# Moving the high part of stationary weights by 64 bytes in SBUF in a four-layer hybrid encoder

## The chip, the cores and the metric

The kernel runs on one core of one Trainium2 chip, in one launch that computes the whole encoder. The metric is the device time of a launch in microseconds (us), lower is better. The core has five engines that run side by side: PE (TensorE, the matrix array), DVE (VectorE), ACT (ScalarE), POOL (GpSimd) and SP (SyncE, which here only issues transfers). PE reads two things from SBUF, the on-chip memory: the stationary operand, which a weight load (PEld in the profile) puts into the array, and the moving operand, which a matmul streams past it. Results go to PSUM.

## What is computed

Four layers over a sequence of 256 rows of width 1024 in fp32. Each layer has a token mixer, a cross-attention over 256 memory rows and an MLP, and after each of the three a LayerNorm of `alpha*h + y`. The mixer is a gated linear recurrence (RG-LRU) in layers 0 and 3, an RWKV-7 delta rule in layer 1 and chunked attention in layer 2. The reference, cut to the trunk:

```python
for i in range(DEPTH):                       # DEPTH = 4
    kind, j = i % N_MIXERS, i // N_MIXERS
    y = (rglru_block, rwkv7_time_mix, chunk_relpos_attention)[kind](h, ...)
    h = _layer_norm(DEEPNORM_ALPHA * h + y, ln_g[i, 0], ln_b[i, 0])
    y = memory_cross_attention(h, mem, mx_w_q[i], mx_w_kv[i], mx_w_o[i])
    h = _layer_norm(DEEPNORM_ALPHA * h + y, ln_g[i, 1], ln_b[i, 1])
    y = squared_relu_mlp(h, mlp_w1[i], mlp_w2[i])      # square(relu(x @ w1)) @ w2
    h = _layer_norm(DEEPNORM_ALPHA * h + y, ln_g[i, 2], ln_b[i, 2])
```

## The kernel before

**Split products.** The large products keep nearly fp32 accuracy with the matrix array's fast fp32r type: every operand x is split into a high part (x rounded to fp32r) and a low part (the rest). A product of two split operands is three matmuls: high by high, low by high, high by low.

**The weight stream.** Weights come from HBM in chunks of 128 partitions by up to 1024 columns. `Stream._dma` (L97) issues the transfer of a chunk into a `wraw` tile on SP's queue, in the order of use. `Stream._split` (L114) makes two tiles of it: `whi`, by a cast on ACT (L471), and `wlo`, by a subtraction on DVE (L472). The pool `hl` holds seven `whi` and seven `wlo` tiles. The instruction order is written out by hand in Python; there is no scheduler.

**Two kinds of product.** Where activations are stationary (`mm_piece`, L289 to L291), the weights move: 512 columns of `whi` or `wlo` a matmul (504 or 336 in the RG-LRU), and every matmul loads 128 columns of activations. Where weights are stationary (`gemm_t` at L347, by `wt_piece`, L310 and L311), the activations move. The tile `ht` holds the transposed activations, first the high parts of both row halves, then the low parts. L310 loads 128 columns of `whi` and streams 512 columns: four runs of 128, high and low parts together. L311 loads 128 columns of `wlo` and streams 256: two runs of 128, the high parts. One after the other they are a **pair**; `gemm_t` makes four chunks into 32 pairs, in groups of 16 (8 and 4 where other work stands between). It serves seven of the eight blocks of the first MLP product in each layer, half of the query product of each cross-attention, and three sixths of the attention's projection: 35 calls, 1120 pairs. In an MLP block the 32 pairs are followed by 48 matmuls of the second MLP product with moving weights (L289 to L291). `wt_steps` (L330) also has stationary weights, for the keys of the memory: it takes 256 columns in every matmul.

**Homes.** By the home of a tile I mean its byte address in a partition. In the built program before, `whi`, `wlo`, `ht`, the activations of the MLP, the memory tiles and nearly all other operands of the fast matmuls have the home 224 modulo 256. Slices begin at multiples of 512 bytes, so that the operands that PE reads together begin at the same place modulo 256. Some small tiles (`mhalf`, `rc`) are wider than their use to keep it so. SBUF is nearly full at the widest stage.

Of the kernel before, what the change touches and what calls it, by code (L numbers as in the profile page):

```python
# [7 lines left out]
F32 = mybir.dt.float32  # L8
F32R = mybir.dt.float32r
# [7 lines left out]
T = 256  # L17
# [3 lines left out]
CT = 126  # L21
# [16 lines left out]
STP = 2  # L38
RW_B = 16
RC_P = 262  # L40
RC_S = 320 + RW_B
# [25 lines left out]
class Stream:  # L67
# [29 lines left out]
    def _dma(self):  # L97
        if self.nd >= len(self.plan):
            return
        k, (name, idx, p, f, _) = self.k, self.plan[self.nd]  # L100
        t = k.raw_p.tile([128, 1024], F32, name="wraw", tag="wraw")
        src = k.I[name]
        for i in idx:
            src = src[i]
        for c in self._cols(self.nd, f):
            k.nc.sync.dma_start(t[:p, c], src[:, c])
        self.raw[self.nd] = t
        self.nd += 1
# [5 lines left out]
    def _split(self):  # L114
# [3 lines left out]
        while self.nd <= i:  # L118
            self._dma()
        _, _, p, f, whole = self.plan[i]  # L120
        raw = self.raw.pop(i)
        if whole:
            self.hl[i] = raw
            self.ns += 1
            return
        hi = k.hl_p.tile([128, 1024], F32R, name="whi", tag="whi")
        lo = k.hl_p.tile([128, 1024], F32R, name="wlo", tag="wlo")
# [30 lines left out]

    def take(self, name, idx, p, f, whole=False):
        key = (name, tuple(idx), p, f, whole)  # L160
        if self.k.dry:
            self.plan.append(key)
            return 0
        i = self.pos
        assert self.plan[i] == key, (self.plan[i], key)
        self.pos += 1
        while self.ns <= i:
            self._split()
        return i
# [74 lines left out]
class Kern:  # L244
# [9 lines left out]

    def chunks(self, name, idx, n, p, f):
        if self.gb_due is not None:
            self.gb_due -= 1
            if self.gb_due == 0:
                if self.ln_i == 0:
                    for t in range(2):  # L260
                        self.nc.sync.dma_start(self.h[t], self.I["x"][t * 128:(t + 1) * 128, :])
                self.load_gb()
        return [self.st.take(name, (*idx, q), p, f) for q in range(n)]

# [82 lines left out]
    def gemm_t(self, name, idx, x, banks):  # L347

        ch = self.chunks(name, idx, 4, 128, 1024)
        for m in range(2):  # L350
# [37 lines left out]
    def resid(self, t, nh, acc):  # L388
# [5 lines left out]
        if nh == 0:  # L394
            self.bn[t] = self.sm.tile([128, 2, 6], F32, name="bnst", tag="bnst")
        self.nc.vector.bn_stats(out=self.bn[t][:, nh, :], in_=h[:, sl])
# [160 lines left out]
    def cross(self, l, left):  # L557

        nc, tc = self.nc, self.tc
        with tc.tile_pool(name="cr", bufs=1, reuse_waits="tile") as p:  # L560
# [4 lines left out]
            P, PT, o = {}, {}, {}  # L565
            sums = [self.sm.tile([128, 4], F32, name="ssum", tag="ssum") for _ in range(2)]

# [232 lines left out]
    def lru(self, l, j):  # L800
# [3 lines left out]
        with self.tc.tile_pool(name="lru", bufs=1, reuse_waits="tile") as p:  # L804
# [13 lines left out]
            def x_piece(i):  # L818
                for t, a in self.gemm(*half_in(1, i), 4, self.hT, 128, LW[i]):
                    if i == 0 and t == 0:  # L820
                        x0 = p.tile([128, 2, LW[0]], F32, name="xn", tag="C")
                    s = x0[:, t, :] if i == 0 else gn[t][:, 1008:] if i == 2 else p.tile([128, LW[1]], F32, name="xn", tag=f"B{t}")
                    nc.scalar.copy(s, a[:, :LW[i]])
# [72 lines left out]
            def decay(g):  # L896
                n = tiles[g]
                a, h = ri[g][:, 0], ri[g][:, 1]
                a2 = p.tile([CT, 4, T], F32, name="a2", tag="C")[:, :n, :]
                nc.scalar.activation(a, a, AF.Exp)  # L900
# [261 lines left out]
    def rwkv(self, l, j):  # L1162
# [6 lines left out]
        R2 = r2.enter_context(tc.tile_pool(name="rwb", bufs=1, reuse_waits="tile"))  # L1169
        rc = R2.tile([128, RC_P + 24], F32, name="rc")  # L1170
        nc.sync.dma_start(rc[:, :RC_P], self.I["rw_const"][:, :RC_P])
        cumM, cumX, w3 = rc[:, 0:128], rc[:, 128:256], rc[:, 256:262]
        two = lambda P, n: [P.tile([128, D], F32, name=f"{n}{t}", tag=f"{n}{t}") for t in range(2)]
        r, k, a, s = two(R1, "r"), two(R2, "k"), two(R2, "a"), two(R2, "s")
# [3 lines left out]
        rkrow = R2.tile([128, D], F32, name="rkrow", tag="rkrow")  # L1178
        Dc = R2.tile([128, 8, 8], F32, name="Dc")[:, :3]
        state = [R2.tile([128, 4, 64], F32, name=f"st{f}") for f in range(2)]  # L1180
        hv = lambda x: x.rearrange("p (a b) -> p a b", b=64)
# [458 lines left out]
        def gn(t, f):  # L1640

            cs = slice(f * 512, (f + 1) * 512)
            y = r[t][:, cs]
            mn = self.sm.tile([128, 8], F32, name="gmn", tag="gmn")
            vr = self.sm.tile([128, 8], F32, name="gvr", tag="gvr")
            sq = R2.tile([128, 512], F32, name="gsq", tag=("ptmp", "pi")[f])
# [51 lines left out]
        if not GNP:  # L1698

            S.activation(self.sm.tile([128, 1], F32, name="gone", tag="gone"), self.mhalf[:, 0:1], AF.Sqrt, scale=-1.0)  # L1700
        run(1, elim(0), gram(0, 0), gram(0, 1), pre(1))
        lnxg = self.gb_p.tile([128, D], F32, name="lnxg", tag="g")
        lnxb = self.gb_p.tile([128, D], F32, name="lnxb", tag="b")
# [67 lines left out]
    def run(self):  # L1771
# [14 lines left out]
        with ExitStack() as ctx:  # L1786
# [6 lines left out]
            self.ht_p = P("ht", 1)  # L1793
            self.sm = P("sm", 4)
            self.acc_p = P("acc", 4, space=PSUM)
            self.mm_p = P("mm", 2, space=PSUM)
# [3 lines left out]
            if not self.dry:  # L1800
                make_identity(nc, self.ident[:, :])
            self.mhalf = self.c_p.tile([128, 120], F32, name="mhalf")
            nc.vector.memset(self.mhalf, -0.5)
# [185 lines left out]
```

## Time and profile before

| | |
|---|---|
| median of 3 runs | 1785.25 us |
| lowest and highest | 1781.33 and 1785.4 us |
| the profiled execution | 1786.16 us |
| its span, first to last instruction | 1784.4 us |
| its mean granted TensorE clock | 0.987 |

The profile is of one execution. A row of its groups has source line, engine, operation, result and operands with their shapes, count, then the busy time in us and the mean time of one in ns, then the idle time of the engine just before. A matmul's duration there has its way through the array in it, so matmuls that follow each other overlap; how fast they follow is read from their starts in the timeline. The granted clock is a share of the full 2.4 GHz: 1.00 is that level and 0.50 is 1.2 GHz.

### The profile page before, as it was taken

Reading aid. Unit: us, or ns where it says so; the run is one execution under the profiler, and the core shown is the slowest. Engines: PE = TensorE matmul, PEld = TensorE weight load, DVE = VectorE, ACT = ScalarE, POOL = GpSimd, SP = SyncE. Lnnn points to the kernel's source line nnn. Section 1 sums busy time; section 2 is a strip of 40 time slices with the busy share of each in tenths; the row PEclk is TensorE's granted clock in tenths of the full one; section 3 lists DMA queues with packets and bytes.
Section 4 is the critical chain, followed back from the end, with each engine's and each line's share of the span. In section 5 each row is a group of like instructions: output and inputs, shape, how many; then the busy total and the mean of one; then the engine's idle time right before and its main releaser. Section 6 shows DMA issues by size and latency. Waiting matters only on the chain.

```text
span 1784.4 us, 25405 instructions
## 1 busy us (share of the span) xinstructions
PE 1723.6 (97%) x9944; PEld 1432.5 (80%) x9944; DVE 1248.9 (70%) x1795; ACT 852.4 (48%) x1268; POOL 55.5 (3%) x70
## 2 busy tenths in 40 slices
PE   8989999999999989999999999999999999999998
PEld 6788988888777656888887888888888787988886
DVE  6767676667578698786666666876667777676665
ACT  5754544444444133644443544645444674544442
POOL 3000000000000001000000000000000000000000
PEclk9899999999999999999999999999999999999999
DMA  7365555556342223455556634446554645536552
GB/s 265 102 213 173 189 189 189 189 189 204 95 146 72 96 84 129 143 187 200 188 190 202 238 107 141 148 150 224 188 190 158 225 138 181 201 130 225 190 189 94
DMA packets 92277, 301.11 MB, mean 169 GB/s; under 512 B 11770, under 2 KB 19962, under 8 KB 92028
## 3 DMA queue, kind: packets, MB, share of 16 engines
q1 hardware_dynamic: 92156, 299.48, 49.7%
q8 instruction: 78, 1.28, 0.3%
q14 instruction: 43, 0.35, 0.1%
HBM read 298.40 MB, written 1.05 MB: 168 GB/s over the span
## 4 chain that ended last, share of the span: by engine, by line
PE 80%; DVE 10%; ACT 4%; DMA 3%; issue 2%; POOL 0%; SPq 0%; DVEq 0%; ACTq 0%
PE acc L291 12%; PE acc L290 12%; PE acc L289 12%; PE tp L310 5%; PE mm L310 5%; PE acc L310 4%; PE acc L533 4%; PE acc L330 4%; PE tp L311 3%; PE mm L311 3%; PE acc L203 2%; PE tp L368 2%; DVE wlo L472 2%; PE acc L311 2%; PE mm L502 1%
## 5 line engine op out<-in xcount | busy, mean ns | idle before, releaser
L472 DVE TENSOR_TENSOR wlo<-wraw,whi 128x1024 fp32r<-128x1024 f32 (+4 forms) x505 | 591.8, 1203 | 145.8 <-ACT whi L471 134.0
L471 ACT CAST whi<-wraw 128x1024 fp32r<-128x1024 f32 (+4 forms) x505 | 507.3, 1035 | 220.4 <-PE acc L291 147.5
L289 PE MATMUL acc<-whi,ahi 128*128 128x512 f32 x512 | 200.3, 391 | 0.0
L291 PE MATMUL acc<-whi,alo 128*128 128x512 f32 x512 | 199.7, 390 | 0.0
L290 PE MATMUL acc<-wlo,ahi 128*128 128x512 f32 x512 | 199.3, 389 | 0.0
L289 PE MATMUL acc<-whi,ht 128*128 128x512 f32 (+2 forms) x368 | 143.3, 389 | 5.5 <-ACT whi L471 5.5
L290 PE MATMUL acc<-wlo,ht 128*128 128x512 f32 (+2 forms) x368 | 141.5, 384 | 3.9 <-DVE wlo L472 3.9
L291 PE MATMUL acc<-whi,ht 128*128 128x512 f32 (+2 forms) x368 | 141.5, 385 | 1.7 <-DVE ht L372 1.7
L310 PE MATMUL tp<-ht,whi 128*128 128x512 f32 x384 | 136.7, 398 | 0.0
L310 PE MATMUL mm<-ht,whi 128*128 128x512 f32 x384 | 136.5, 398 | 0.0
L310 PE MATMUL acc<-ht,whi 128*128 128x512 f32 x352 | 126.0, 400 | 2.2 <-DVE qkT L1011 2.2
L291 PEld LDWEIGHTS acc<-whi,alo 128*128 128x128 f32 x512 | 96.1, 188 | 20.9
L289 PEld LDWEIGHTS acc<-whi,ahi 128*128 128x128 f32 x512 | 96.1, 188 | 20.1
L290 PEld LDWEIGHTS acc<-wlo,ahi 128*128 128x128 f32 x512 | 96.2, 188 | 19.2
L311 PE MATMUL tp<-ht,wlo 128*128 128x256 f32 x384 | 107.9, 281 | 0.0
L311 PE MATMUL mm<-ht,wlo 128*128 128x256 f32 x384 | 107.8, 281 | 0.0
L311 PE MATMUL acc<-ht,wlo 128*128 128x256 f32 x352 | 98.6, 280 | 0.0
L759 DVE TENSOR_TENSOR rel<-mm,rel 128x256 f32<-128x256 f32 x48 | 18.6, 425 | 110.4 <-ACT rel L758 110.4
L763 ACT CAST ahi<-rel 128x512 fp32r<-128x512 f32 x56 | 34.8, 622 | 110.2 <-DVE rel L762 110.2
L289 PEld LDWEIGHTS acc<-whi,ht 128*128 128x128 f32 x368 | 70.6, 192 | 20.1 <-ACT whi L471 6.2
L310 PEld LDWEIGHTS tp<-ht,whi 128*128 128x128 f32 x384 | 72.2, 188 | 18.0
L310 PEld LDWEIGHTS mm<-ht,whi 128*128 128x128 f32 x384 | 72.2, 188 | 17.6
(395 smaller groups left out, 3318.3 us busy)
## 6 DMA issues: line engine op xcount, KB each, us to landing
wraw<-in_w SPq DMA_DIRECT2D x256, 512.0 KB, 4.7
wraw<-in_w_kv SPq DMA_DIRECT2D x64, 512.0 KB, 4.6
wraw<-in_w_q SPq DMA_DIRECT2D x32, 512.0 KB, 4.3
wraw<-in_w_co SPq DMA_DIRECT2D x32, 512.0 KB, 4.6
wraw<-in_lru_in SPq DMA_DIRECT2D x31, 504.0 KB, 4.8
wraw<-in_ca_qkv SPq DMA_DIRECT2D x24, 512.0 KB, 4.8
wraw<-in_lru_out SPq DMA_DIRECT2D x20, 512.0 KB, 6.0
ln_gt<-in_ln_g SPq DMA_DIRECT2D x12, 512.0 KB, 6.5
```

Source lines behind the costliest of these rows:

```text
L203: return f(*a, **k)
L289: nc.tensor.matmul(acc[:, :w], lhsT=a, rhs=wh[:p, ws], start=s, stop=False)
L290: nc.tensor.matmul(acc[:, :w], lhsT=a, rhs=wl[:p, ws], start=False, stop=False)
L291: nc.tensor.matmul(acc[:, :w], lhsT=b, rhs=wh[:p, ws], start=False, stop=e)
L310: self.nc.tensor.matmul(four, lhsT=wh[:, ws], rhs=xy, start=s, stop=False)
L311: self.nc.tensor.matmul(four[:, :2], lhsT=wl[:, ws], rhs=x, start=False, stop=e)
L330: self.nc.tensor.matmul(a, lhsT=w[:, ws], rhs=v, start=s and i == 0, stop=e and i == 2)
L368: self.nc.tensor.transpose(dst_ps[:n, j * p:(j + 1) * p], s, self.ident[:p, :p])
L471: self.nc.scalar.copy(hi, src)
L472: self.nc.vector.tensor_tensor(out=lo, in0=src, in1=hi.bitcast(F32), op=ALU.subtract)
L533: nc.tensor.matmul(a, lhsT=u, rhs=w[:, ws], start=s, stop=e)
L763: nc.scalar.copy(hi[:, sl, :], r)
```

## The change

`take`, `chunks` and the plan of the stream carry a new number, `shift`. `gemm_t` passes 16, all others 0. `_split` makes the `whi` tile 1088 columns wide in place of 1024 and takes the 1024 columns from `shift` on: with 16 fp32 columns that is 64 bytes further. `wlo` is left as it is. A `whi` tile is then 4352 bytes, 17 times 256, so the tiles' own homes stay at 224 modulo 256. In the built program `whi` stands at 32 modulo 256 for the 140 chunks of `gemm_t` and at 224 for the others; `wlo`, `ht` and the rest of the fast operands stay at 224.

The seven wider tiles take 1792 bytes more in each partition. To make room, small tiles share homes: in the RG-LRU the tile `xn` of the first piece takes the home of `B0`, the next ones move to `B1` and `B2`, and `a2` takes the home of the gate weights `gw0`; in the RWKV layer the constants `rc` and the state share the tag `st` and the state is made later; `mhalf`, `Dc` and the LayerNorm statistics get smaller or fewer tiles; `ssum`, `gmn` and `gvr` take the tags of other small tiles. `rc`, `Dc` and the state then stand at 96 modulo 256.

The diff:

```diff
--- before.py
+++ after.py
@@ -37,6 +37,7 @@
 ST0 = 3
 STP = 2
 RW_B = 16
+DCP = 32
 RC_P = 262
 RC_S = 320 + RW_B
 PE_SHARE = .4,.4,.4,.4
@@ -97,7 +98,7 @@
     def _dma(self):
         if self.nd >= len(self.plan):
             return
-        k, (name, idx, p, f, _) = self.k, self.plan[self.nd]
+        k, (name, idx, p, f, *_) = self.k, self.plan[self.nd]
         t = k.raw_p.tile([128, 1024], F32, name="wraw", tag="wraw")
         src = k.I[name]
         for i in idx:
@@ -117,13 +118,13 @@
         k, i = self.k, self.ns
         while self.nd <= i:
             self._dma()
-        _, _, p, f, whole = self.plan[i]
+        _, _, p, f, whole, shift = self.plan[i]
         raw = self.raw.pop(i)
         if whole:
             self.hl[i] = raw
             self.ns += 1
             return
-        hi = k.hl_p.tile([128, 1024], F32R, name="whi", tag="whi")
+        hi = k.hl_p.tile([128, 1088], F32R, name="whi", tag="whi")[:, shift:shift + 1024]
         lo = k.hl_p.tile([128, 1024], F32R, name="wlo", tag="wlo")
         w = f // 2
         if _pitch(w) == w or f <= 512:
@@ -156,8 +157,9 @@
         if not self.k.dry and self.ns == self.last + self.hl_bufs:
             self._split()
 
-    def take(self, name, idx, p, f, whole=False):
-        key = (name, tuple(idx), p, f, whole)
+    def take(self, name, idx, p, f, whole=False, shift=0):
+
+        key = (name, tuple(idx), p, f, whole, shift)
         if self.k.dry:
             self.plan.append(key)
             return 0
@@ -252,7 +254,7 @@
         self.st = Stream(self, [] if self.dry else plan, 4, 7)
 
 
-    def chunks(self, name, idx, n, p, f):
+    def chunks(self, name, idx, n, p, f, shift=0):
         if self.gb_due is not None:
             self.gb_due -= 1
             if self.gb_due == 0:
@@ -260,7 +262,7 @@
                     for t in range(2):
                         self.nc.sync.dma_start(self.h[t], self.I["x"][t * 128:(t + 1) * 128, :])
                 self.load_gb()
-        return [self.st.take(name, (*idx, q), p, f) for q in range(n)]
+        return [self.st.take(name, (*idx, q), p, f, shift=shift) for q in range(n)]
 
     def mm_piece(self, acc, chunks, lhs, p, w, kpc=2, kt0=0, start=True, stop=True, last=False, near=None, tail=None):
 
@@ -346,7 +348,7 @@
 
     def gemm_t(self, name, idx, x, banks):
 
-        ch = self.chunks(name, idx, 4, 128, 1024)
+        ch = self.chunks(name, idx, 4, 128, 1024, shift=16)
         for m in range(2):
             accs = [banks[m](), banks[m]()]
             self.wt_piece(accs, ch, x.both, m, last=m == 1)
@@ -392,7 +394,7 @@
             out=h[:, sl], in0=h[:, sl], scalar=ALPHA, in1=acc[:, :], op0=ALU.mult, op1=ALU.add
         )
         if nh == 0:
-            self.bn[t] = self.sm.tile([128, 2, 6], F32, name="bnst", tag="bnst")
+            self.bn[t] = self.bn_p.tile([128, 2, 6], F32, name="bnst", tag=f"bnst{t}")
         self.nc.vector.bn_stats(out=self.bn[t][:, nh, :], in_=h[:, sl])
 
     def ln(self, t, aside=None):
@@ -563,7 +565,7 @@
             q = [pair([128, 4, T], f"qh{g}", f"ql{g}") for g in range(2)]
             self.kv_hl = (k, v) = pair([128, 8, T], "kh", "kl"), pair([128, 2, D], "vh", "vl")
             P, PT, o = {}, {}, {}
-            sums = [self.sm.tile([128, 4], F32, name="ssum", tag="ssum") for _ in range(2)]
+            sums = [self.sm.tile([128, 4], F32, name="ssum", tag="ss") for _ in range(2)]
 
             def take_over(i):
 
@@ -818,8 +820,8 @@
             def x_piece(i):
                 for t, a in self.gemm(*half_in(1, i), 4, self.hT, 128, LW[i]):
                     if i == 0 and t == 0:
-                        x0 = p.tile([128, 2, LW[0]], F32, name="xn", tag="C")
-                    s = x0[:, t, :] if i == 0 else gn[t][:, 1008:] if i == 2 else p.tile([128, LW[1]], F32, name="xn", tag=f"B{t}")
+                        x0 = p.tile([128, 2, LW[0]], F32, name="xn", tag="B0")
+                    s = x0[:, t, :] if i == 0 else gn[t][:, 1008:] if i == 2 else p.tile([128, LW[1]], F32, name="xn", tag=f"B{t + 1}")
                     nc.scalar.copy(s, a[:, :LW[i]])
                     nat[i, t] = s
                     if i and t == 0:
@@ -896,7 +898,7 @@
             def decay(g):
                 n = tiles[g]
                 a, h = ri[g][:, 0], ri[g][:, 1]
-                a2 = p.tile([CT, 4, T], F32, name="a2", tag="C")[:, :n, :]
+                a2 = p.tile([CT, 4, T], F32, name="a2", tag="gw0")[:, :n, :]
                 nc.scalar.activation(a, a, AF.Exp)
                 nc.scalar.activation(a2, a, AF.Square)
                 nc.vector.scalar_tensor_tensor(out=h, in0=a2, scalar=1.0, in1=h, op0=ALU.add, op1=ALU.mult)
@@ -1167,17 +1169,17 @@
         r1, r2 = ExitStack(), ExitStack()
         R1 = r1.enter_context(tc.tile_pool(name="rwa", bufs=1, reuse_waits="tile"))
         R2 = r2.enter_context(tc.tile_pool(name="rwb", bufs=1, reuse_waits="tile"))
-        rc = R2.tile([128, RC_P + 24], F32, name="rc")
+        rc = R2.tile([128, RC_P], F32, name="rc", tag="st")
         nc.sync.dma_start(rc[:, :RC_P], self.I["rw_const"][:, :RC_P])
         cumM, cumX, w3 = rc[:, 0:128], rc[:, 128:256], rc[:, 256:262]
+        Dc = R2.tile([128, DCP], F32, name="Dc")[:, :24].rearrange("p (c q) -> p c q", c=3)
         two = lambda P, n: [P.tile([128, D], F32, name=f"{n}{t}", tag=f"{n}{t}") for t in range(2)]
         r, k, a, s = two(R1, "r"), two(R2, "k"), two(R2, "a"), two(R2, "s")
         g2 = R1.tile([128, D], F32, name="g2")
         tg = R1.tile([128, T], F32, name="tg")
         bs = [R1.tile([128, 16], F32, name=f"bs{t}") for t in range(2)]
         rkrow = R2.tile([128, D], F32, name="rkrow", tag="rkrow")
-        Dc = R2.tile([128, 8, 8], F32, name="Dc")[:, :3]
-        state = [R2.tile([128, 4, 64], F32, name=f"st{f}") for f in range(2)]
+        state = []
         hv = lambda x: x.rearrange("p (a b) -> p a b", b=64)
         bc = lambda x, p=128: x.unsqueeze(2).to_broadcast([p, 8, 64])
         half = lambda c: slice(64 * c, 64 * c + 64)
@@ -1641,8 +1643,8 @@
 
             cs = slice(f * 512, (f + 1) * 512)
             y = r[t][:, cs]
-            mn = self.sm.tile([128, 8], F32, name="gmn", tag="gmn")
-            vr = self.sm.tile([128, 8], F32, name="gvr", tag="gvr")
+            mn = self.sm.tile([128, 8], F32, name="gmn", tag="nm")
+            vr = self.sm.tile([128, 8], F32, name="gvr", tag="rs")
             sq = R2.tile([128, 512], F32, name="gsq", tag=("ptmp", "pi")[f])
             V.tensor_reduce(mn, hv(y), AX.X, ALU.add)
             V.tensor_scalar(mn, mn, -1.0 / 64, None, ALU.mult)
@@ -1699,6 +1701,8 @@
 
             S.activation(self.sm.tile([128, 1], F32, name="gone", tag="gone"), self.mhalf[:, 0:1], AF.Sqrt, scale=-1.0)
         run(1, elim(0), gram(0, 0), gram(0, 1), pre(1))
+        st2 = R2.tile([128, 2, 4, 64], F32, name="st", tag="st")
+        state += [st2[:, f] for f in range(2)]
         lnxg = self.gb_p.tile([128, D], F32, name="lnxg", tag="g")
         lnxb = self.gb_p.tile([128, D], F32, name="lnxb", tag="b")
         nc.sync.dma_start(lnxg, self.I["rw_lnx_g"][j].partition_broadcast(128))
@@ -1792,6 +1796,7 @@
             self.gb_p = P("gb", 1)
             self.ht_p = P("ht", 1)
             self.sm = P("sm", 4)
+            self.bn_p = P("bn", 1)
             self.acc_p = P("acc", 4, space=PSUM)
             self.mm_p = P("mm", 2, space=PSUM)
             self.tp_p = P("tp", 2, space=PSUM)
@@ -1799,7 +1804,7 @@
             self.ident = self.c_p.tile([128, 128], F32, name="ident")
             if not self.dry:
                 make_identity(nc, self.ident[:, :])
-            self.mhalf = self.c_p.tile([128, 120], F32, name="mhalf")
+            self.mhalf = self.c_p.tile([128, 56], F32, name="mhalf")
             nc.vector.memset(self.mhalf, -0.5)
             self.hT = _LazyT(self)
             self.h = [self.c_p.tile([128, D], F32, name=f"h{t}") for t in range(2)]
```

On every engine the instructions stand in the same order before and after, with the same shapes (the one other width is `mhalf`'s, a memset of 120 columns that becomes 56). What differs in the built program beside addresses is a few waits that come from the shared homes: four on ACT before exponentials of the cross-attention, three on POOL in the RWKV layer, and one on SP. The one on SP stands in the second RG-LRU layer (layer 3), where SP's queue carries the gate weights `gw`, the memory `kT`, a LayerNorm's rows and then the weight chunks `wraw`. Before:

```order
L106 DMA wraw<-in_lru_in 128x1008 [waits DMAHW2_49,DVE_49]
L865 DMA gw<-in_lru_gw 128x1512 [waits PE_49] x2
L865 DMA gw<-in_lru_gw 128x2x504
L459 DMA kT<-in_memT 128x8x128
L459 DMA kT<-in_memT 128x8x128 [waits DMAHW3_49]
```

The same place on SP after:

```order
L107 DMA wraw<-in_lru_in 128x1008 [waits DMAHW2_49,DVE_49]
L867 DMA gw<-in_lru_gw 128x1512 [waits PE_49] x2
L867 DMA gw<-in_lru_gw 128x2x504 [waits PE_49]
L461 DMA kT<-in_memT 128x8x128
L461 DMA kT<-in_memT 128x8x128 [waits DMAHW3_49]
```

Nothing has moved; the third transfer of gate weights now waits for a matmul as the first two do. In the built program that is the last matmul of L622 in the cross-attention of layer 2.

## Rows read from the trace of the kernel before

**Rows 1.** The page's busy shares of the engines over the span.

```profile
PE 1723.6 (97%) x9944; PEld 1432.5 (80%) x9944; DVE 1248.9 (70%) x1795; ACT 852.4 (48%) x1268; POOL 55.5 (3%) x70
```

**Rows 2.** The page's chain that ended last, by engine.

```profile
PE 80%; DVE 10%; ACT 4%; DMA 3%; issue 2%; POOL 0%; SPq 0%; DVEq 0%; ACTq 0%
```

**Rows 3.** One MLP block, 379.4 to 401.6 us: busy time of each engine.

```profile
core 0: us, PE busy (x) PEld busy (x) DVE busy (x) ACT busy (x) POOL busy (x), PEclk, DMA share, GB/s
379.40:401.60 22.20, 22.20 (x114) 18.77 (x113) 13.71 (x17) 10.38 (x15) 0.00 (x0) 1.00 0.56 190
```

**Rows 4.** The page's groups of the pairs (busy us, mean ns of one | idle).

```profile
L310 PE MATMUL tp<-ht,whi 128*128 128x512 f32 x384 | 136.7, 398 | 0.0
L310 PE MATMUL mm<-ht,whi 128*128 128x512 f32 x384 | 136.5, 398 | 0.0
L310 PE MATMUL acc<-ht,whi 128*128 128x512 f32 x352 | 126.0, 400 | 2.2 <-DVE qkT L1011 2.2
```

**Rows 5.** PE's timeline in one MLP block: start us, duration us, instruction.

```profile
366.87 0.39 PE L290 MATMUL acc<-wlo,ahi 128*128 128x512 f32 x1
...
368.00 0.39 PE L310 MATMUL mm<-ht,whi 128*128 128x512 f32 x1
368.23 0.28 PE L311 MATMUL mm<-ht,wlo 128*128 128x256 f32 x1
368.34 0.40 PE L310 MATMUL mm<-ht,whi 128*128 128x512 f32 x1
368.57 0.28 PE L311 MATMUL mm<-ht,wlo 128*128 128x256 f32 x1
368.69 0.40 PE L310 MATMUL mm<-ht,whi 128*128 128x512 f32 x1
368.93 0.28 PE L311 MATMUL mm<-ht,wlo 128*128 128x256 f32 x1
369.05 0.40 PE L310 MATMUL mm<-ht,whi 128*128 128x512 f32 x1
369.29 0.28 PE L311 MATMUL mm<-ht,wlo 128*128 128x256 f32 x1
369.40 0.40 PE L310 MATMUL mm<-ht,whi 128*128 128x512 f32 x1
...
379.29 0.40 PE L289 MATMUL acc<-whi,ahi 128*128 128x512 f32 x1
...
390.23 0.39 PE L310 MATMUL mm<-ht,whi 128*128 128x512 f32 x1
```

**Rows 6.** PE's timeline, matmuls of 256 columns alone; 50 starts lie between.

```profile
178.38 0.28 PE L330 MATMUL acc<-memlo,whi 128*128 128x256 f32 x1
...
184.38 0.28 PE L330 MATMUL acc<-memhi,whi 128*128 128x256 f32 x1
```

**Rows 7.** Granted clock and busy time of 746 to 751 us.

```profile
746.00:751.00 5.00, 5.00 (x24) 4.97 (x24) 5.00 (x5) 3.07 (x4) 0.00 (x0) 0.50 0.51 154
```

**Rows 8.** PE's timeline there; 21 starts lie between the last two rows.

```profile
745.53 0.55 PE L622 MATMUL mm<-qh,vh 128*128 128x256 f32 x1 [1.45 <-DVE ql L372]
...
746.41 0.41 PE L622 MATMUL mm<-qh,vl 128*128 128x256 f32 x1
...
750.89 0.41 PE L622 MATMUL mm<-qh,vl 128*128 128x256 f32 x1
```

**Rows 9.** PE's timeline: the gate matmuls, plain fp32, four passes of 256 columns each.

```profile
1405.19 1.03 PE L877 MATMUL mm<-xc,gw 127*126 127x256 f32 x4
...
1415.62 1.03 PE L877 MATMUL mm<-xc,gw 127*126 127x256 f32 x4
```

**Rows 10.** SP's timeline in layer 3, and PE's in the cross-attention before.

```profile
1168.64 0.28 PE L622 MATMUL mm<-qh,vl 128*128 128x256 f32 x1
...
1386.99 1.62 SPq L865 DMA_DIRECT2D gw<-in_lru_gw  x3
```

## The prediction, made before the changed kernel ran

> **What bounds the kernel now.** I read the page's busy shares first, then its chain, then one MLP block by stages, then PE's timeline. PE is busy for 97% of the span, DVE for 70%, ACT for 48% [rows 1], and the chain that ended last is PE for 80% [rows 2]. The shares are averages, so the stage that the change touches must be read by itself. In an MLP block PE is busy for all of 22.20 us, while DVE needs 13.71, ACT 10.38 and the transfers 0.56 of the DMA engines' time [rows 3]. No other engine is near its limit there, and the pairs wait for almost nothing: 2.2 us in all in front of the 1120 L310 (384 and 384 and 352) [rows 4]. So in these stages the end moves by what PE's pace gains or loses, in full: a pair that gets 1 ns shorter is worth 1.1 us.
>
> The pace is in the starts [rows 5]. Matmuls of 512 moving columns with activations as weights follow each other 226 ns apart: five between 366.87 and 368.00. Then 32 pairs run from 368.00 to 379.29, 352.8 ns each. Their steps are not even: the first pair takes 0.34 us, the next 0.35, 0.36, 0.35. The 48 matmuls that follow take 10.94 us, 227.9 ns each, 1.9 ns over 226: the unevenness is carried into them for a little. Matmuls of 256 columns alone follow at 120.0 ns: 50 starts in 6.00 us [rows 6]. A pair is one of 512 and one of 256, so by these paces it should take 346 ns. It takes 352.8. **6.8 ns of a pair are lost to something that neither kind suffers alone.**
>
> What is it? At a granted clock of 0.50, the 1.2 GHz level, matmuls of 256 columns follow at 213.3 ns, 4.48 us for 21, with their weights loaded beside them as always [rows 7, 8]; PE had waited 1.45 us for DVE ahead of that stretch [rows 8]. Twice as fast would be 106.7 ns; at 1.00 it is 120.0. So 13.3 ns come on top at the full clock, and a fixed number of array cycles is not the reason, since at the lower clock it would then cost more, and it costs nothing. Something that does not get faster with the array is met only when columns stream at the full clock. The weight load that runs beside each matmul and reads SBUF at the same time is the candidate. If two readers meet, then it can matter where each stands, and in every fast matmul both now stand at the same home modulo 256.
>
> **The change part by part.**
>
> *The shift.* It touches one load out of two in a pair: the load of `whi`, which runs beside L311. The load of `wlo` beside L310 keeps its relation to `ht`. No row of before has a fast matmul whose load stands 64 bytes off, so its price has to be bounded. From below: half of the overhead cannot be touched, because it belongs to the load of `wlo`. The fastest that L311 could stream is 106.7 ns [rows 7, 8], with L310 at 226 [rows 5]: 333 ns a pair, 20 less than now, times 1120 is -22 us. A nearer row is the first pair of a group, which starts from an undisturbed stream and takes 340 ns [rows 5]: -12.8 x 1120 = -14.3 us. Nearer still is the pace of both kinds alone, 346 ns: -6.8 x 1120 = -7.6 us. From above: the loss could happen twice, 6.8 ns more, +7.6 us. I take 346 ns. The even streams are the commonest state in this trace, they come from readers that keep one relation from matmul to matmul, and the pairs differ from them in that their unequal lengths let the relation wander; a fixed quarter turn between `whi` and `ht` would keep the two from starting on the same place. I do not take 340: it is seen only where nothing lay before.
>
> *The carry into the MLP's second product.* If the pairs run evenly, the 1.9 ns on each of 48 matmuls go as well, 0.09 us a block, 28 blocks: -2.6 us at most [rows 5]. Part of it may be waiting of another kind, so I count a quarter, -0.6 us.
>
> *Writing and reading the shifted tile.* ACT's cast and DVE's subtraction write and read it in the same shapes. If they changed pace, the block has 8.5 us of room on DVE and 11.8 on ACT [rows 3]: nothing.
>
> *The shared homes.* All engines keep their order. The new waits name instructions of an earlier stage. The one on a queue that matters is SP's: the third load of gate weights at about 1387 us now waits for a matmul that started at 1168.64 us [rows 10], 218 us before, so neither it nor the memory's rows and the weight chunks queued behind it on SP start later. The waits on ACT and POOL are of the same kind, on uses at least a sub-layer back: nothing. If one of them were late, it would show as an idle time of the engine, and it would have to exceed a microsecond to be measured.
>
> *Sum.* -7.6 - 0.6 = -8.2 us from the profiled execution's 1786.2 us gives 1778.0. The median of the runs is 0.9 us lower than that execution, so against the median it is 1777.1.
>
> **The Trainium skill against this.** The trace says 120.0 ns at the full clock where the lower one would make it 106.7 [rows 6 to 8]. "TensorE: Matmul & The Clock Gate", in "Step-by-step: what each phase is for", says that PE has two independent read ports, so that loading the next weights takes no read bandwidth from the running matmul, and "SBUF — State Buffer", in "Who interferes with whom", that PE never waits on anyone. By that rule a home could not matter, and the sum would be nought. The rows do not decide it: an overhead at the full clock is there, but no row ties it to an address.
>
> **The rivals.**
>
> *No change.* The overhead belongs to swapping weights at the full clock and not to where they stand. For it: plain fp32 matmuls load the gate weights from homes that lie between 224 and 56 modulo 256 in the built program, against a moving operand at 224, and four passes take 1.03 us with either end [rows 9]. There the home is of no account. Against it: those passes stream 256 columns in some 215 ns, half the pace, where the overhead is not met either; and a cost of swapping would not explain why a pair of unequal lengths loses 6.8 ns more. The time is then the median's, 1785.3 us. This is also what the skill's rule gives.
>
> *More than forecast.* The load of `whi` no longer meets the stream at all: 340 ns or less, -14.3 us to -22 us, 1771 to 1763 us. For it: the first pair of a group does it [rows 5]. Against it: a stream that passes 512 bytes of weights at twice their speed crosses their place somewhere in any case.
>
> *Slower.* The same home is the good relation: both readers start together, the stream is ahead at once and stays clear for the longest time. With `whi` 64 bytes ahead, the stream runs into the load just after the start of L311, in every pair. For it: 226 and 120 ns, the even paces, are all reached with equal homes [rows 5, 6]. Against it: the pairs have equal homes as well and are uneven. The price is one more loss a pair: it decides from the point where L311 takes over 120 ns as a mean, which no other work hides since PE is never idle there, and 6.8 ns x 1120 is +7.6 us: 1792.9 us.
>
> **How the numbers follow.** About 0.3%, 5.4 us, is what a measurement of this kernel can tell from no change. Forecast: 0.42, at 1777. No change: 0.27, at 1785. More: 0.14. Slower: 0.17, at 1793. Faster by over 0.3% means under 1779.9; it gets the case "more" and all of the forecast but its weak end, where pairs lose half of the excess, 0.06: 0.50. Within 0.3%: no change and that weak end, with a little of "slower" that costs less than a loss a pair: 0.35. Slower: 0.15. The range reaches from the middle of "more" to the lower part of "slower": 1766 to 1790 us. What it leaves out is the far half of either, some 0.18.
>
> **What will show it.** Forecast: 32 pairs of an MLP block take 11.1 us in place of 11.29, evenly spaced, L310 226 and L311 120 ns apart, and a block 22.0 us. No change: the starts are those of before. "More": L311 under 114 ns as a rule. Slower: L310 near 240 ns in every pair. If pairs gain and the end does not, PE must show idle time in the MLP or other streams must have become slower; the streams with moving weights should stay at 226 ns since their homes are what they were. The forecast is wrong in its ground if the pairs change by some other amount than multiples of the 6.8 ns that I see lost, or if anything outside the pairs moves the end by over 2 us.

## The result and the profile after

| | before | after |
|---|---|---|
| median, runs side by side | 1783.29 us (4 runs) | 1773.13 us (4 runs) |
| lowest and highest | 1779.85 and 1785.4 us | 1770.86 and 1774.74 us |
| the profiled execution | 1786.16 us | 1772.77 us |
| its span | 1784.4 us | 1771.0 us |

The ratio is 0.9939, with a 95% interval of 0.9926 to 0.9951: the kernel got faster by 10.2 us, 0.6%. The forecast was 1777.1 us, from 1785.25.

The page of after, its busy shares (against [rows 1]) and its groups of the pairs (against [rows 4]; what were L310 and L311 are now L312 and L313, and L289 to L291 are L291 to L293):

```profile
PE 1708.2 (96%) x9944; PEld 1425.9 (81%) x9944; DVE 1248.5 (70%) x1795; ACT 851.8 (48%) x1268; POOL 54.6 (3%) x70
...
L312 PE MATMUL mm<-ht,whi 128*128 128x512 f32 x384 | 132.1, 390 | 0.0
L312 PE MATMUL tp<-ht,whi 128*128 128x512 f32 x384 | 131.7, 389 | 0.0
L312 PE MATMUL acc<-ht,whi 128*128 128x512 f32 x352 | 125.2, 398 | 2.3 <-DVE qkT L1013 2.3
```

PE lost 15 us of busy time, the other engines next to nothing, and the wait ahead of the pairs is 2.3 us as it was 2.2. The two groups of the MLP fell from 398 to 390 and 389 ns a matmul; the third group, `acc`, which holds the pairs of the cross-attention, of layer 2's attention and of the first transposed block of each MLP, from 400 to 398 only. So most of the gain has a place: the other blocks of the MLP.

PE's timeline of after in the same MLP block as [rows 5] (start us, duration us, instruction):

```profile
364.07 0.40 PE L312 MATMUL mm<-ht,whi 128*128 128x512 f32 x1
364.31 0.28 PE L313 MATMUL mm<-ht,wlo 128*128 128x256 f32 x1
364.43 0.39 PE L312 MATMUL mm<-ht,whi 128*128 128x512 f32 x1
364.65 0.28 PE L313 MATMUL mm<-ht,wlo 128*128 128x256 f32 x1
364.77 0.39 PE L312 MATMUL mm<-ht,whi 128*128 128x512 f32 x1
364.99 0.28 PE L313 MATMUL mm<-ht,wlo 128*128 128x256 f32 x1
365.11 0.39 PE L312 MATMUL mm<-ht,whi 128*128 128x512 f32 x1
...
374.97 0.40 PE L291 MATMUL acc<-whi,ahi 128*128 128x512 f32 x1
...
385.87 0.40 PE L312 MATMUL mm<-ht,whi 128*128 128x512 f32 x1
```

After a first pair of 0.36 us by these rows (354 ns in the trace) each pair takes 0.34, without the pattern 0.35, 0.36, 0.35 of before. The 32 pairs take 10.90 us, 340.6 ns each (before 352.8). Both steps of a pair became shorter: from the starts in ns of all 24 such chains, without the first four pairs of each, the step from the 512 columns to the 256 took 236.2 ns before and 226.6 after, the step from the 256 to the next 512 took 117.0 and 113.4. The 48 matmuls behind them take 10.90 us, 227.1 ns each (before 227.9). The block lasts 21.80 us instead of 22.23. There are 24 such blocks, six a layer: 24 x 0.43 = 10.3 us, near the 10.2 us between the medians (8.7 to 13.2 by the interval). The 352 pairs outside these blocks gained some 2 us more where both profiles had the full clock; the interval holds the blocks alone as well as all pairs together.

The profiled executions differ by 13.4 us, 3 more than the medians. Part of that is the clock: by the mean granted clock, before spent 46.0 us of its span at the lower level, after 34.3. Windows of before and then of after, 60 to 85 us and 960 to 980 us; the third number from the end is the granted clock:

```profile
60.00:85.00 25.00, 25.00 (x93) 19.16 (x94) 14.16 (x16) 17.59 (x21) 0.00 (x0) 0.81 0.22 68
960.00:980.00 20.00, 19.97 (x111) 16.71 (x109) 10.22 (x11) 8.28 (x11) 0.00 (x0) 1.00 0.75 241
```

```profile
60.00:85.00 25.00, 25.00 (x115) 20.48 (x115) 16.56 (x20) 20.98 (x25) 0.00 (x0) 1.00 0.22 70
960.00:980.00 20.00, 17.73 (x97) 15.41 (x97) 10.24 (x13) 8.53 (x12) 0.00 (x0) 0.91 0.78 249
```

Before ran part of the first stretch at the lower level and did 93 matmuls there where after did 115; in the second the clock was the other way round. Such stretches come and go from one execution to the next (a later execution of the changed kernel, shown at the end of the experiments, had 0.77 in the first stretch), so two profiles are best compared stage by stage, and only where both have a clock of 1.00, as in the block above.

Not every group of pairs gained. The pairs of the cross-attention come in groups of 16, 8 and 4 behind other work. PE's timeline of after for one of 16:

```profile
169.70 0.39 PE L312 MATMUL acc<-ht,whi 128*128 128x512 f32 x1
169.93 0.28 PE L313 MATMUL acc<-ht,wlo 128*128 128x256 f32 x1
170.04 0.40 PE L312 MATMUL acc<-ht,whi 128*128 128x512 f32 x1
170.28 0.28 PE L313 MATMUL acc<-ht,wlo 128*128 128x256 f32 x1
170.40 0.39 PE L312 MATMUL acc<-ht,whi 128*128 128x512 f32 x1
...
175.30 1.03 PE L370 MATMUL tp<-ident,P 128*128 128x128 f32 x8
```

Its first pair takes 0.34 us, but the next 0.36, and the 16 take 5.60 us, 350 ns each (353 before). In two layers the second 16 pairs of the MLP's first transposed block even went from 352 to 358 ns a pair. The loss is not gone from the kernel; in the long chains the pairs no longer fall into it.

### The profile page after: what moved, and what is told of

It is laid out like the page before. It is cut to its first block, busy times and chain, and to the rows that moved or that the text cites. A ratio compares the mean times of both kernels' runs of the same rounds, so it can differ in the third digit from the quotient of the medians.

```text
span 1771.0 us, 25412 instructions
## 1 busy us (share of the span) xinstructions
PE 1708.2 (96%) x9944; PEld 1425.9 (81%) x9944; DVE 1248.5 (70%) x1795; ACT 851.8 (48%) x1268; POOL 54.6 (3%) x70
## 4 chain that ended last, share of the span: by engine, by line
PE 79%; DVE 10%; ACT 4%; DMA 3%; issue 2%; POOL 1%; SPq 0%; DVEq 0%; ACTq 0%; POOLq 0%
PE acc L293 12%; PE acc L291 12%; PE acc L292 12%; PE mm L312 5%; PE tp L312 5%; PE acc L312 4%; PE acc L535 4%; PE acc L332 4%; PE mm L313 2%; PE tp L313 2%; PE acc L205 2%; PE tp L370 2%; DVE wlo L474 2%; PE acc L313 2%; PE mm L504 1%
## 5 line engine op out<-in xcount | busy, mean ns | idle before, releaser
L291 PE MATMUL acc<-whi,ahi 128*128 128x512 f32 x512 | 199.8, 390 | 0.0
L293 PE MATMUL acc<-whi,alo 128*128 128x512 f32 x512 | 199.2, 389 | 0.0
L291 PE MATMUL acc<-whi,ht 128*128 128x512 f32 (+2 forms) x368 | 142.8, 388 | 5.6 <-ACT whi L473 5.6
L293 PE MATMUL acc<-whi,ht 128*128 128x512 f32 (+2 forms) x368 | 141.1, 383 | 1.7 <-DVE ht L374 1.7
L312 PE MATMUL mm<-ht,whi 128*128 128x512 f32 x384 | 132.1, 390 | 0.0
L312 PE MATMUL tp<-ht,whi 128*128 128x512 f32 x384 | 131.7, 389 | 0.0
L312 PE MATMUL acc<-ht,whi 128*128 128x512 f32 x352 | 125.2, 398 | 2.3 <-DVE qkT L1013 2.3
L293 PEld LDWEIGHTS acc<-whi,alo 128*128 128x128 f32 x512 | 96.1, 188 | 20.2
L291 PEld LDWEIGHTS acc<-whi,ahi 128*128 128x128 f32 x512 | 96.1, 188 | 20.1
L313 PE MATMUL mm<-ht,wlo 128*128 128x256 f32 x384 | 106.1, 276 | 0.0
L313 PE MATMUL tp<-ht,wlo 128*128 128x256 f32 x384 | 106.0, 276 | 0.0
L313 PE MATMUL acc<-ht,wlo 128*128 128x256 f32 x352 | 98.7, 280 | 0.0
L292 PEld LDWEIGHTS acc<-wlo,ht 128*128 128x128 f32 x368 | 70.3, 191 | 21.7 <-DVE wlo L474 9.6
L291 PEld LDWEIGHTS acc<-whi,ht 128*128 128x128 f32 x368 | 70.3, 191 | 19.8 <-ACT whi L473 6.3
L312 PEld LDWEIGHTS mm<-ht,whi 128*128 128x128 f32 x384 | 72.1, 188 | 15.3
```

The lines of the kernel that those rows point to most:

```text
L291: nc.tensor.matmul(acc[:, :w], lhsT=a, rhs=wh[:p, ws], start=s, stop=False)
L292: nc.tensor.matmul(acc[:, :w], lhsT=a, rhs=wl[:p, ws], start=False, stop=False)
L293: nc.tensor.matmul(acc[:, :w], lhsT=b, rhs=wh[:p, ws], start=False, stop=e)
L312: self.nc.tensor.matmul(four, lhsT=wh[:, ws], rhs=xy, start=s, stop=False)
L313: self.nc.tensor.matmul(four[:, :2], lhsT=wl[:, ws], rhs=x, start=False, stop=e)
```

## The experiments

Two theories stood against each other. **P** is that of the prediction: what counts is where a load stands against the columns that stream beside it, at a price for each load. **D** came up on the way: what counts is how the two loads of a pair stand to each other. A single execution tells little (those of before in these experiments lie from 1781 to 1789 us), so where a kernel ran only once the verdict rests on the pairs in the timeline, where 1 ns can be told.

**Only the homes.** The shared homes and the wider tile, without the shift:

```diff
-        ch = self.chunks(name, idx, 4, 128, 1024, shift=16)
+        ch = self.chunks(name, idx, 4, 128, 1024, shift=0)
```

> The changed kernel with a shift of 0: all the shared homes and the wider tile of the high part stay, only the 64 bytes are taken back. Theory P (place: the pair's pace is set by where the load of the high part stands to the moving operand modulo 256): the pairs of an MLP block fall back to 352.8 ns, the block to 22.2 us, and the time to within 0.3% of the kernel before. Rival H (homes: the gain comes from the other addresses that moved, or from the wider tiles): pairs stay at 340 to 341 ns, block 21.8 us, some 10 us faster than before.

Measured: 1785.03 us against 1785.15 for before, ratio 1.0003 (0.9992 to 1.0015). PE's timeline, the starts of a chain, of the matmuls behind it, and of the next chain:

```profile
368.99 0.39 PE L312 MATMUL mm<-ht,whi 128*128 128x512 f32 x1
...
380.28 0.40 PE L291 MATMUL acc<-whi,ahi 128*128 128x512 f32 x1
...
391.23 0.39 PE L312 MATMUL mm<-ht,whi 128*128 128x512 f32 x1
```

11.29 us for 32 pairs, 352.8 ns, and a block of 22.24 us: the kernel of before. New waits, shared homes and wider tiles cost and bring nothing that the interval tells (3 us at most); the gain is the shift's.

**Other distances.** The same line with 8, 32, 48 and 64 fp32 columns, which is 32, 128, 192 and 256 bytes.

> The changed kernel with a shift of 32 bytes. If the relation counts in units of 64 bytes with two kinds of places (even and odd multiples), 32 bytes stands across the border: pairs between 340 and 353 ns. If it counts in units of 32 bytes: pairs at 340 ns (as 64) or at 352 ns (as 0), block 21.8 or 22.2 us, time 10 us faster or as before.

> The changed kernel with a shift of 128 bytes. Theory P in its simplest form (only equal homes are bad): pairs 340 to 341 ns as with 64, block 21.8 us, some 10 us faster than before. Rival (a certain distance is wanted, a quarter of 256): the pairs stay uneven at 346 to 353 ns, block 22.0 to 22.2 us, 0 to 5 us faster.

> The changed kernel with a shift of 192 bytes, which is 64 bytes behind instead of ahead. Only equal homes are bad: pairs 340 to 341 ns, block 21.8 us, some 10 us faster than before. Direction counts (the load must stand ahead of the moving operand by a little, so that the faster stream meets it late): pairs 346 to 360 ns, block 22.0 to 22.5 us, from 5 us faster to 7 us slower.

> The changed kernel with a shift of 256 bytes in place of 64. Theory P modulo 256: the same relation as no shift, pairs 352.8 ns, block 22.2 us, time as before. Rival: the relation counts over a longer distance than 256 bytes, or any shift breaks the uneven pattern: pairs 340 to 341 ns, block 21.8 us, some 10 us faster.

| `whi` further by | a pair in the MLP | MLP block | time (one run) |
|---|---|---|---|
| 0 bytes | 352.9 ns | 22.23 us | 1785.03 us (median) |
| 32 | 351.1 | 22.13 | 1781.48 |
| 64 | 340.5 | 21.80 | 1773.13 (median) |
| 128 | 351.6 | 22.20 | 1784.34 |
| 192 | 340.5 | 21.80 | 1767.85 |
| 256 | 352.9 | 22.23 | 1783.38 |

PE's timelines with 128 and then with 192 bytes, as above:

```profile
368.59 0.40 PE L312 MATMUL mm<-ht,whi 128*128 128x512 f32 x1
...
379.84 0.40 PE L291 MATMUL acc<-whi,ahi 128*128 128x512 f32 x1
...
390.79 0.40 PE L312 MATMUL mm<-ht,whi 128*128 128x512 f32 x1
```

```profile
363.86 0.40 PE L312 MATMUL mm<-ht,whi 128*128 128x512 f32 x1
...
374.76 0.40 PE L291 MATMUL acc<-whi,ahi 128*128 128x512 f32 x1
...
385.66 0.40 PE L312 MATMUL mm<-ht,whi 128*128 128x512 f32 x1
```

A shift of 256 is as none, and of the distances tried 64 and 192 help. Halfway to 64 there is hardly anything, and 128 is nearly as bad as nothing, so it is not equal homes alone that are bad, as P in its simplest form had it. It does not matter either whether `whi` stands 64 bytes ahead or behind.

**The other load.** `wlo` shifted by 64 bytes, `whi` not:

```diff
-        hi = k.hl_p.tile([128, 1088], F32R, name="whi", tag="whi")[:, shift:shift + 1024]
-        lo = k.hl_p.tile([128, 1024], F32R, name="wlo", tag="wlo")
+        hi = k.hl_p.tile([128, 1024], F32R, name="whi", tag="whi")
+        lo = k.hl_p.tile([128, 1088], F32R, name="wlo", tag="wlo")[:, shift:shift + 1024]
```

> The low part is shifted by 64 bytes and the high part is not (the wide tile is wlo's). What the first four runs showed: 64 and 192 bytes on the high part give pairs of 340.5 ns in the MLP, 0, 128 and 256 give 351.6 to 352.9. Theory S (only the load beside the short matmul, that of whi beside L311's 256 columns, is in the way, since a long matmul has room for either order): nothing is gained, pairs 352 ns, block 22.2 us, time as before. Rival L (any load counts: each matmul loses on its own load's relation): L310 loses less, pairs 340 to 346 ns, block 21.8 to 22.0 us, 5 to 10 us faster than before.

Measured: 1776.61 us (before beside it 1785.07). PE's timeline:

```profile
366.43 0.39 PE L312 MATMUL mm<-ht,whi 128*128 128x512 f32 x1
366.66 0.28 PE L313 MATMUL mm<-ht,wlo 128*128 128x256 f32 x1
366.77 0.40 PE L312 MATMUL mm<-ht,whi 128*128 128x512 f32 x1
...
377.52 0.40 PE L291 MATMUL acc<-whi,ahi 128*128 128x512 f32 x1
...
388.45 0.39 PE L312 MATMUL mm<-ht,whi 128*128 128x512 f32 x1
```

11.09 us for 32 pairs, 346.6 ns: half of the gain, so theory S has fallen. A shift of either load helps, so neither load is the guilty one. But it helps less than the 192 bytes on `whi`, although in both kernels `whi` stands 192 bytes from `wlo`, modulo 256. By P, both shifted should give both gains; by D, they should give nothing, since the two would stand alike again.

**Both loads.** One tile for both, each 64 bytes further, so that every load keeps the distance from `ht` that helped it alone:

```diff
-        hi = k.hl_p.tile([128, 1088], F32R, name="whi", tag="whi")[:, shift:shift + 1024]
-        lo = k.hl_p.tile([128, 1024], F32R, name="wlo", tag="wlo")
+        whl = k.hl_p.tile([128, 2112], F32R, name="whl", tag="whl")
+        hi, lo = whl[:, shift:shift + 1024], whl[:, 1024 + shift:2048 + shift]
```

> High and low part of the stationary weights both stand 64 bytes further (they share one wide tile, so that it needs no more room; order and waits are those of the changed kernel). So far: high part alone 340.5 ns a pair, low part alone 346.6, none 352.9. Theory A (each load loses by its own relation to the moving operand, and the gains add): 333 to 336 ns, MLP block 21.6 us, 4 to 8 us faster than the changed kernel. Rival D (what counts is that the two loads of a pair stand differently, so that the relation alternates as the lengths do): both shifted alike is as none, 350 to 353 ns, block 22.2 us, 10 us slower than the changed kernel.

And with `whi` 192 and `wlo` 64 bytes further, each at a place that is good alone, but 128 apart:

```diff
+        lo, hi = whl[:, shift:shift + 1024], whl[:, 1024 + 3 * shift:2048 + 3 * shift]
```

> High part 192 bytes further, low part 64. Theory A: gains add, 333 to 336 ns a pair. Rival D: the two loads stand 128 bytes apart, which behaves as equal did (a shift of 128 gave 351.6 ns): 350 to 353 ns, block 22.2 us, 10 us slower than the changed kernel.

Measured: 1782.46 and 1783.57 us (before beside them 1785.83). PE's timeline of the first, and then of the second:

```profile
370.25 0.40 PE L312 MATMUL mm<-ht,whl 128*128 128x512 f32 x1
370.48 0.28 PE L313 MATMUL mm<-ht,whl 128*128 128x256 f32 x1
370.60 0.39 PE L312 MATMUL mm<-ht,whl 128*128 128x512 f32 x1
...
381.54 0.40 PE L291 MATMUL acc<-whl,ahi 128*128 128x512 f32 x1
...
392.49 0.40 PE L312 MATMUL mm<-ht,whl 128*128 128x512 f32 x1
```

```profile
367.94 0.40 PE L312 MATMUL mm<-ht,whl 128*128 128x512 f32 x1
...
379.24 0.39 PE L291 MATMUL acc<-whl,ahi 128*128 128x512 f32 x1
...
390.16 0.40 PE L312 MATMUL mm<-ht,whl 128*128 128x512 f32 x1
```

11.29 and 11.30 us, 353 ns a pair in both, and blocks of 22.24 and 22.22 us. Two shifts that each help alone give nothing together. P with a price for each load falls. D holds in part: in the chains of the MLP a pair is long (351.6 to 353.3 ns) wherever its two loads stand 0 or 128 bytes apart modulo 256, and shorter in all three kernels where they stand 64 or 192 apart. But the distance of the loads is not all that counts. With `whi` 192 bytes further and with `wlo` 64 bytes further the two stand alike to each other, and a pair takes 340.5 ns in the one and 346.6 in the other; what differs modulo 256 is where they stand against `ht`.

**The moving weights too.** If 64 bytes between high and low part were good by itself, then all weights should have it. Here the high part of every chunk is shifted, also of those that stream while activations are loaded (one line in `_split`):

```diff
+        shift = 16
```

> All high parts are shifted by 64 bytes, those of the moving weights too (L291 to L293 and, with 256 moving columns, L332). Theory M (the streams with one relation in all their matmuls are already in the best state, since their excess of 13 ns does not depend on the home): 512 moving columns stay at 226 to 227 ns and the time is that of the changed kernel, 1773 us, within 3 us. Rival (every full-clock stream loses by equal homes): 512 moving columns fall by some 7 ns in two of three matmuls, 2400 matmuls, 10 to 16 us faster than the changed kernel; or they rise by as much, 10 to 16 us slower.

Measured: 1794.69 us (before beside it 1785.07), PE's timeline with two chains and the 48 matmuls between them:

```profile
370.77 0.40 PE L313 MATMUL mm<-ht,whi 128*128 128x512 f32 x1
...
381.66 0.39 PE L292 MATMUL acc<-whi,ahi 128*128 128x512 f32 x1
...
392.85 0.39 PE L313 MATMUL mm<-ht,whi 128*128 128x512 f32 x1
...
404.05 0.40 PE L292 MATMUL acc<-whi,ahi 128*128 128x512 f32 x1
```

The 48 matmuls take 11.19 us, 233.1 ns each in place of 227, so theory M has fallen: what is good for pairs is bad for equal lengths. Over all matmuls of 512 columns but the pairs' that is 18 us more than before where both profiles have the full clock, of which the pairs give back 6.5. And of the two chains the first runs at 340.3 ns a pair, the second at 350 (11.20 us), with the same homes modulo 256. So these homes do not fix the pace by themselves. In all 24 chains the step just before tells which it will be: 233 or 234 ns ahead of a chain at 340, 226 to 228 ahead of one at 350. That points to what the chain finds when it starts; what that is no run shows.

The last kernel of this kind gives all weights, the moving ones too, both parts 64 bytes further, so that one relation holds from matmul to matmul again:

> Both parts of all weights stand 64 bytes further, the moving ones too. With only the high parts shifted everywhere, the 512-column streams of moving weights rose from 227 to 233 ns. Theory U (a stream of one length wants one and the same relation in all its matmuls, whichever it is): 227 ns again. Rival E (streams of moving weights want equal homes): 233 to 240 ns, 20 us and more slower than the changed kernel.

Measured: 1787.7 us (before beside it 1785.83, a difference that single runs don't tell). PE's timeline:

```profile
370.85 0.40 PE L313 MATMUL mm<-ht,whl 128*128 128x512 f32 x1
...
382.15 0.39 PE L292 MATMUL acc<-whl,ahi 128*128 128x512 f32 x1
...
393.14 0.40 PE L313 MATMUL mm<-ht,whl 128*128 128x512 f32 x1
```

Pairs take 353 ns, and the 48 matmuls 10.99 us, 229 ns each. Most of the 6 ns come back, so neither theory U (227 ns) nor rival E (233 and more) had it in full. In equal lengths it is mainly the change of relation that costs, and 64 bytes between stream and load, held steady, costs some 2 ns.

**192 beside 64.** The fastest single run was the one with 192 bytes, so it was timed beside the changed kernel, six runs of each on one chip.

> The whi of the pairs stands 192 bytes further (48 floats) in place of 64. Theory D (only the relation of the two loads of a pair counts, and 192 is 64 the other way round): pairs of the MLP 340.5 ns and blocks of 21.80 us, as with 64. If the groups of 16 pairs keep running at 340 to 347 ns, as one look showed, in place of 341 to 359, 112 pairs or so gain about 10 ns each: 1 to 2 us; together with the start of the kernel 1768 us +-2, ratio to the kernel before 0.990 to 0.992. Rival: the one look was chance, and the time is that of 64 bytes, 1773 us, ratio 0.994.

> The changed kernel itself beside the one with 192 bytes, on the same chip: 1773 us, ratio to the kernel before 0.994. Theory D says the MLP is alike in both; what differs between the two lies in the groups of 16 pairs that start behind other work, at most 2 us, or outside the pairs.

Measured: 1769.49 us with 192 (ratio 0.9912, 0.9896 to 0.9929) and 1774.88 us with 64 (0.9936, 0.9921 to 0.9951); before 1786.0. The intervals overlap a little. The MLP is alike in both, 21.80 us a block. The groups of 16 pairs take 340, 341 and 346 ns a pair with 192, and 350, 341 and 346 or 358 with 64: 0.15 to 0.35 us a layer, near 1 us in all. The two profiled spans differ by 10.8 us, 1764.0 against 1774.8, and most of that is the clock: 23.7 us at the lower level with 192, 47.6 with 64. Windows of 60 to 85 us, with 192 and then with 64:

```profile
60.00:85.00 25.00, 25.00 (x116) 20.54 (x115) 16.57 (x20) 21.65 (x25) 0.00 (x0) 1.00 0.21 70
```

```profile
60.00:85.00 25.00, 24.49 (x86) 18.25 (x87) 13.34 (x15) 17.60 (x21) 0.00 (x0) 0.77 0.16 47
```

At 85 us the kernel with 64 is already 7.7 us behind. After had 1.00 there at 64 bytes, so this is no property of the distance that these runs show. 192 bytes is the fastest version measured; that it beats 64 by more than the 1 us that the pairs account for stays open.

## Why the prediction was right, and where it was not

*The place of the gain was right.* PE is never idle in an MLP block, and the pairs gave their gain to the end in full: 24 x 0.43 us by the blocks against 10.2 by the medians. The kernel with only the homes shows that the terms put at nothing for them (the shared homes, the new waits with SP's [rows 10]) were nothing: 1.0003. The two engines that write and read the shifted tile kept their busy time (DVE 1248.9 and 1248.5 us, ACT 852.4 and 851.8). The 50 and 21 starts of [rows 6] and [rows 8] are steps from the first row to the last, so 120.0 and 213.3 ns stand.

*The size of the pair term was wrong.* I counted 346 ns a pair, because "340 is seen only where nothing lay before". It is 340.5 over whole chains of 32, 12.4 ns less than before instead of 6.8. L312 came to 226.6 ns as forecast, and L313 to 113.4 in place of 120; under 114 the prediction had named as the sign of the rival "more than forecast". The row that I set aside, the first pair of a chain at 0.34 us [rows 5], was the nearer bound: chains of 32 can keep that pace. The measured gain of 10.2 us lay between the 7.6 and the 14.3 of these two rows, since not all 1120 pairs got it. The 768 of the 24 blocks gained 12.4 ns each, 9.5 us; of the 352 others, some groups stayed near 350 or became slower, and together they gained some 2 us.

*The carry* was put at 0.6 us; by the blocks it is 22.23 - 11.29 = 10.94 us against 10.90, 0.04 us x 24 = 0.9 us. Right in kind and near in size.

*The ground was wrong*, and the prediction had said what would show it: pairs that change by something other than multiples of 6.8 ns. I took the overhead as a meeting of one stream with one load, at a price for each load. The runs show no such price: both loads 64 bytes from where they were take 353 ns, like none. I also counted the shift as touching only the load of `whi`, beside the 256 columns; but 9.6 ns of the gain in the even part of a chain came in the step of the 512 columns, beside which the unmoved `wlo` is loaded, and 3.6 in the other. That `wlo` was left in place was not half a measure, as my bound of 333 ns supposed ("half of the overhead cannot be touched"); moved along by the same 64 bytes it takes the gain away. So that the forecast came near, -8.2 us against -10.2, was in part luck: the place and the direction were right, the reason for 346 ns was not.

*The rivals.* "No change" has fallen: the kernel with and without the shift differ in the place of one operand, 340.5 against 352.9 ns a pair. The rule of the Trainium skill ("TensorE: Matmul & The Clock Gate", "Step-by-step: what each phase is for") says that loading the next weights takes no SBUF read bandwidth from the running matmul. What the prediction drew from it, that a home could not matter, has fallen by these numbers; the rule itself no run tests, since none shows whether the loss arises at SBUF's ports or elsewhere on the way to the array. The plain fp32 matmuls that spoke for "no change" [rows 9] run at half the pace, as the prediction had noted against them. "Slower" rested on equal homes being the good relation. For equal lengths it is the best relation tried (227 ns, against 229 with all weights shifted and 233 with the high parts alone); for pairs of 512 and 256 columns it is not. I had seen both kinds in [rows 5] and [rows 6] and did not think that they could want opposite things.

*What stays open* is the mechanism. Both loads moved alike by 64 bytes is as if `ht` had moved against them, and changed nothing (353 ns); but with the loads apart, their place against `ht` was worth 6 ns. No theory on record gives both, and no run moved `ht` alone or `wlo` by another distance than 64 bytes. Nor is it shown why a pair wants its relation to change from matmul to matmul where equal lengths want it to stay, or what a chain meets at its start that puts it at 340 or at 350 ns.

## What to carry to other kernels

Where PE never waits, compare the spacing of starts with the best spacing that the same shape shows anywhere in the trace, even once: here an uneven pattern with a short first step was a loss that could be had back, and the short step came near its size. Where such matmuls alternate between two lengths, try the two stationary operands 64 or 192 bytes apart modulo 256, and move first the one that the longer matmul uses (`whi` here, 12.4 ns a pair against 6.2 for `wlo`); leave streams of one length with one relation throughout. Try one operand at a time, and both together: here the gains of each alone did not add.

## What the runs showed of the hardware

- With the granted clock at 1.00 the pace of back-to-back fp32r matmuls depends on the SBUF addresses of their operands modulo 256: 340.5 to 353 ns for a pair of 512 and 256 columns, 227 to 233 ns for 512 columns alone.
- The dependence is not gradual: moving `whi` by 32 bytes gives 1.8 ns of a pair, 64 gives 12.4, 128 gives 1.3, 192 gives 12.4, 256 nothing.
- It is not one load's own place that counts. Both loads moved alike by 64 bytes: 353 ns. High and low part 64 or 192 bytes apart: pairs faster by 12.4 ns with `whi` moved and by 6.2 with `wlo` moved; streams of 512 with the high part moved by 64 slower by 6 ns.
- A chain of the same matmuls with the same homes modulo 256 can run at 340 or at 350 ns a pair, as a mean over its 32 pairs.
